# Feed forward on 512 moving columns: gate and up by tokens, down past one load for both parts, and a pad of 96 bytes

## The chip, the core and the metric

The kernel runs on one core of a Trainium2 chip. TensorE multiplies matrices and accumulates in PSUM; VectorE, ScalarE and GpSimd work on elements; 16 DMA engines move data from HBM into SBUF. The metric is the device time of one execution in microseconds, the median over several. In the profiles PE is TensorE's matmuls, PEld its loads of the stationary operand, DVE VectorE, ACT ScalarE, POOL GpSimd, SP the engine that issues the DMAs. A difference in this kernel's time under about 0.2% can't be told from none.

## The reference, cut to what matters

Two blocks of two layers each work on 256 tokens of 1024 features. The mixers (attention, recurrences, long convolutions) differ; each of the four layers ends with a gated feed forward of 2816 hidden features. In block 1, where `ffn_w_up` holds the gate's columns and then up's:

```python
hf = rmsnorm(x, norm_ffn)
gate, up = jnp.split(hf @ ffn_w_up, 2, axis=-1)
return x + (jax.nn.silu(gate) * up) @ ffn_w_down
```

Block 2 computes `(silu(u @ w1) * (u @ w3)) @ w2`, with u the modulated norm, and adds it times a gate per feature. All is float32.

## The kernel before, in words

The stream `xT` stands feature-major: 128 partitions, 8 tiles of features, 256 tokens. A float32 product is made of three products in the format fp32r: the weights are split into a high part `wh` (a ScalarE cast, L471) and a low part `wl` (a VectorE subtract, L472), the activations likewise, and `mm3` (L484 to L487) adds `wh` by high, `wh` by low and `wl` by high.

`weights` (L456) brings the weights in units of 512 KB: 4 blocks of 128 rows by 256 columns, into four buffers for what is loaded and three each for `wh` and `wl`. The layout of the weights in HBM is made in `layout` from the table TILES.

`s_tiles` (L489) computes 256 columns of weights for 256 tokens in one bank of PSUM: for each block k of 128 rows and each half of the columns, `mm3` with the 128 x 128 weights loaded and the 256 tokens moving. So every matmul of the feed forward moves 256 columns and has a load of its own. `t_form` (L508) is the other way round, tokens loaded and 256 weights' columns moving.

`ffn` (L537) runs over 11 tiles of 256 hidden features: gate into one bank, up into another, silu on ScalarE (L559), the product on VectorE (L560), and a split into `ph` and `pl` (L453, L454), feature-major already. In block 1 the norm's factor of each token is broadcast over the partitions (`pb`) and both products are multiplied by it (L555). In block 2 the first tile comes ready from `ffn_ahead`. Then four tiles of 256 output features: 22 blocks of hidden features, the same three products, and `residual` (L571 to L577) adds each half, 256 columns, to `xT`. Three banks of PSUM (tag mm) are shared by all of these.

The order on each engine is not the order of the code: the framework lays the whole program out by a simulated timeline and puts on each engine's queue what it thinks ready first, so work of other stages (in block 1 the contexts of block 2, called by `beside`) stands between the feed forward's matmuls.

Of the kernel before, what the change touches and what calls it, by code (L numbers as in the profile page):

```python
# [15 lines left out]
OP = mybir.AluOpType  # L16
# [106 lines left out]
def _dft():  # L123
    """Transforms at the frequencies pi (2 k + 1) / 512, k = 0..127 and then 255..128, of signals about 127.5 (F, and
    back: G) and, for k < 128, of the even and the odd places of the filters (H)."""
# [20 lines left out]
def _positions():  # L146
    """What the filters take of their places: the even ones, then the odd ones."""
# [27 lines left out]
def _run(c0, n, w=256):  # L175
    return [(c, [(c, w)]) for c in range(c0, c0 + n * w, w)]


# the weights in tiles of columns, which name or first column leads to: [pieces: first column or None, columns]
# [4 lines left out]
    "w_lift": _run(0, 4), "w_out": _run(0, 4), "ffn_w_up": _run(0, 22), "ffn_w_down": _run(0, 4),  # L184
# [3 lines left out]
    "ffn_w1_2": _run(0, 11), "ffn_w3_2": _run(0, 11), "ffn_w2_2": _run(0, 4),  # L188
# [11 lines left out]
def _unit(cols):  # L200
    """How many blocks of 128 rows one load brings, of how many columns at most."""
    return (KU, 256) if cols > 128 else (2 * KU, 128)


def layout(inputs):
    """The inputs as the chip loads them: vectors as columns, weights by tiles and units of rows, tokens turned."""
# [11 lines left out]
    for name in ("x", "mem", "ctx_2"):  # L218
        out[name + "_T"] = np.ascontiguousarray(inputs[name][0].reshape(S, KT, 128).transpose(2, 1, 0)).reshape(128, KT * S)
    for name, tiles in TILES.items():  # L220
# [3 lines left out]
        for _, pieces in tiles:  # L224
            cut = [w[:, :, c:c + n] if c is not None else np.zeros(w.shape[:2] + (n,), w.dtype) for c, n in pieces]
            t = cut[0] if len(cut) == 1 else np.concatenate(cut, 2)
            step = 256 if name == "mod_w_2" else _unit(t.shape[2])[0] * 128
# [8 lines left out]
class Halves:  # L236
    """Two [128, 4, tokens] tiles as one [128, 8, tokens]."""
# [13 lines left out]
class K:  # L251
# [22 lines left out]
    def pump(self, n=1):  # L274
        """Emit some of the work that waits to be laid between the matrix products."""
        self.due += n * self.rate
        while self.bg is not None and self.due >= 1:
            self.due -= 1
            self.pump_one()
# [57 lines left out]
    def later(self, *dst):  # L337
        """Whatever is loaded into dst waits until the first products are on their way."""
# [7 lines left out]
    def rstd_tokens(self, src, r, lp):  # L346
        """1 / rms of every token, per token, in r [128, 2]."""
# [9 lines left out]
    def rstd(self, src, pt):  # L357
        """1 / rms of every token, per token, with pt's first columns for the sums."""
# [43 lines left out]
    def s_ahead(self, u, at, bank="mm", mws=((0, 128), (128, 128)), t=None):  # L402
        """The tile that s_tiles gives, from what is ahead of the norm; in SBUF."""
# [23 lines left out]
    def norm_ahead(self, u, src, bank="aux2"):  # L427
        """The norm itself, after what is ahead of it."""
# [27 lines left out]
    def weights(self, name, i, key, kt=KT):  # L456
        """A function of k that gives high and low parts of rows k * 128.. of a tile; k must not go down."""
# [30 lines left out]

    def s_tiles(self, ps, at, xh, xl, kt=KT, first=True, last=True, x0=0, mws=((0, 128), (128, 128)), k0=0):  # L489
        """ps [m, 256 tokens each] += (columns m0..m0 + mw of the weights)^T x.  # L490

        Where sums of one bank are built up side by side only the bank's first product starts and only its
        last one stops."""
# [33 lines left out]
    def ffn_ahead(self, u, l, w_gate, w_up, u0, lp):  # L527
        """The first tile of the gated products."""
# [8 lines left out]
    def ffn(self, xh, xl, l, w_gate, w_up, u0, w_down, gcol=None, first=None, scale=None):  # L537
        nc = self.nc
        with self.pool("ffn") as fp:
            ph = fp.tile([128, FT, S], F32R, name="ph")  # L540
            pl = fp.tile([128, FT, S], F32R, name="pl")
            for i in range(FFN // 256):
# [3 lines left out]
                else:  # L546
                    pg = self.mm()
                    self.s_tiles(pg, self.weights(w_gate, l, i * 256), xh, xl)
                    pu = self.mm()
                    self.s_tiles(pu, self.weights(w_up, l, u0 + i * 256), xh, xl)  # L550
                    sg = fp.tile([128, 512], F32, tag="f1", bufs=2, name="f1")
                    pr = fp.tile([128, 512], F32, tag="f2", bufs=2, name="f2")
                    if scale is not None:
                        for o, ps in ((sg, pg), (pr, pu)):
                            nc.vector.tensor_tensor(o.rearrange("p (m t) -> p m t", m=2),  # L555
# [1688 lines left out]
```

## Time and profile before

| | |
|---|---|
| median of 3 runs | 2064.69 us (2064.21 to 2064.89) |
| span of the profiled execution (the only time that the page gives of it) | 2068.7 us |
| TensorE busy (16,666 matmuls) | 2030.9 us, 98% |
| VectorE, ScalarE busy | 1506.7 us (73%), 1033.8 us (50%) |
| chain that ended last | TensorE 92% |

The span is that of an execution under the profiler, 4.0 us above the median. Busy time counts a matmul's record from start to end; the records overlap, so the time that one matmul takes of the queue is the distance between two starts, which a count over a stretch gives. The feed forwards lie at about 431 to 660 us (with other work between), 1029 to 1286 (likewise), 1587 to 1742 and 1884 to 2059.

### The profile page before, as it was taken

To read this page: it belongs to the slowest core of one execution; us is meant where nothing else is said; L and a number is where in the kernel's file an instruction comes from. 1 tells how busy PE (TensorE), PEld (TensorE's weight loads), DVE (VectorE), ACT (ScalarE), POOL (GpSimd) and SP (SyncE) were. 2 spreads that over 40 slices of the span, in tenths; PEclk is the share of its full clock that TensorE was granted. 3 is DMA by queue.
4 is the path that set the end of the run, shared out by engine and by line. 5 is a ranking of instruction groups with operands and counts; after the bars stand their busy time and mean duration, and the time that the engine had idled before them with its cause. 6 is when DMAs were issued, how large, how long until landed. Compare 5 with 4: busy or idle time off the path is not lost.

```text
span 2068.7 us, 40596 instructions
## 1 busy us (share of the span) xinstructions
PE 2030.9 (98%) x16666; PEld 1931.3 (93%) x16666; DVE 1506.7 (73%) x2491; ACT 1033.8 (50%) x1604; POOL 86.7 (4%) x80
## 2 busy tenths in 40 slices
PE   8999999999999999999999999999989999999998
PEld 8999999999999989999999989897779999899998
DVE  6968877896866868977767855885667556897554
ACT  6553355565544664454655434662135445656443
POOL 0000000010000000000000001000010000001001
PEclk9999999999999999999999999997999999999999
DMA  8754564865567755747644534452215666545654
GB/s 323 273 179 156 201 204 167 319 244 193 185 220 241 239 169 174 243 144 263 201 160 145 175 109 141 164 159 80 67 47 177 194 187 222 163 133 176 190 176 132
DMA packets 118561, 379.34 MB, mean 183 GB/s; under 512 B 18239, under 2 KB 28776, under 8 KB 117096
## 3 DMA queue, kind: packets, MB, share of 16 engines
q1 hardware_dynamic: 118376, 376.76, 55.2%
q8 instruction: 130, 2.13, 0.4%
q14 instruction: 55, 0.45, 0.1%
HBM read 366.27 MB, written 10.25 MB: 182 GB/s over the span
## 4 chain that ended last, share of the span: by engine, by line
PE 92%; DVE 2%; ACT 2%; issue 2%; DMA 1%; POOL 0%; SPq 0%; DVEq 0%; POOLq 0%; ACTq 0%
PE mm L487 22%; PE mm L485 22%; PE mm L486 22%; PE mm L522 1%; PE mm L521 1%; PE mm L523 1%; PE aux L1233 1%; DVE wl L472 1%; PE aux L1758 1%; ACT wh L471 1%; PE aux L1085 1%; PE aux L1763 1%; PE aux L823 1%; PE aux L858 1%; PE aux L2094 1%
## 5 line engine op out<-in xcount | busy, mean ns | idle before, releaser
L471 ACT CAST wh<-w 128x1024 fp32r<-128x1024 f32 (+2 forms) x570 | 589.0, 1035 | 680.5 <-PE mm L486 521.7
L472 DVE TENSOR_TENSOR wl<-w,wh 128x1024 fp32r<-128x1024 f32 (+2 forms) x570 | 686.2, 1205 | 305.8 <-ACT wh L471 303.4
L485 PE MATMUL mm<-hh,wh 128*128 128x256 f32 (+1 forms) x1776 | 505.6, 285 | 1.3 <-ACT wh L471 0.7
L487 PE MATMUL mm<-hh,wl 128*128 128x256 f32 (+1 forms) x1776 | 504.1, 284 | 1.0 <-DVE wl L472 1.0
L486 PE MATMUL mm<-hl,wh 128*128 128x256 f32 (+1 forms) x1776 | 504.2, 284 | 0.0
L485 PEld LDWEIGHTS mm<-hh,wh 128*128 128x128 f32 (+1 forms) x1776 | 335.8, 189 | 6.0 <-issue 3.6
L487 PEld LDWEIGHTS mm<-hh,wl 128*128 128x128 f32 (+1 forms) x1776 | 335.7, 189 | 5.5 <-issue 3.3
L486 PEld LDWEIGHTS mm<-hl,wh 128*128 128x128 f32 (+1 forms) x1776 | 335.8, 189 | 3.9 <-issue 2.6
L485 PE MATMUL mm<-xh,wh 128*128 128x256 f32 x960 | 270.6, 283 | 1.0 <-ACT uc L422 0.9
L487 PE MATMUL mm<-xh,wl 128*128 128x256 f32 x960 | 269.5, 282 | 1.6 <-DVE wl L472 1.5
L486 PE MATMUL mm<-xl,wh 128*128 128x256 f32 x960 | 270.3, 283 | 0.2
L487 PE MATMUL mm<-ph,wl 128*128 128x256 f32 x704 | 197.9, 281 | 0.0
L485 PE MATMUL mm<-ph,wh 128*128 128x256 f32 x704 | 197.7, 281 | 0.0
L486 PE MATMUL mm<-pl,wh 128*128 128x256 f32 x704 | 197.4, 280 | 0.0
L487 PEld LDWEIGHTS mm<-xh,wl 128*128 128x128 f32 x960 | 182.2, 190 | 5.2 <-issue 2.5
L485 PEld LDWEIGHTS mm<-xh,wh 128*128 128x128 f32 x960 | 181.1, 189 | 4.1 <-issue 2.2
L486 PEld LDWEIGHTS mm<-xl,wh 128*128 128x128 f32 x960 | 180.5, 189 | 3.8 <-issue 3.0
L1227 DVE SCALAR_TENSOR_TENSOR macc<-mw,cs,macc 128x512 f32<-128x512 f32 x196 | 146.2, 752 | 10.8 <-DMA mw<-in_t_mod_w 10.2
L487 PEld LDWEIGHTS mm<-ph,wl 128*128 128x128 f32 x704 | 132.7, 189 | 1.9 <-issue 1.9
L485 PEld LDWEIGHTS mm<-ph,wh 128*128 128x128 f32 x704 | 132.4, 188 | 1.6 <-issue 1.5
L486 PEld LDWEIGHTS mm<-pl,wh 128*128 128x128 f32 x704 | 132.4, 188 | 1.5 <-issue 1.4
L487 PE MATMUL mm<-brh,wl 128*128 128x256 f32 x384 | 108.3, 283 | 0.0
(679 smaller groups left out, 3607.8 us busy)
## 6 DMA issues: line engine op xcount, KB each, us to landing
w<-in_t_w_in SPq DMA_DIRECT2D x148, 512.0 KB, 4.3
w<-in_t_ffn_w SPq DMA_DIRECT2D x128, 512.0 KB, 4.3
mw<-in_t_mod_w SPq DMA_DIRECT2D x96, 512.0 KB, 4.6
w<-in_t_ffn_w_up SPq DMA_DIRECT2D x88, 512.0 KB, 4.0
w<-in_t_ab_w_in SPq DMA_DIRECT2D x42, 512.0 KB, 4.9
w<-in_t_ffn_w_down SPq DMA_DIRECT2D x40, 512.0 KB, 3.6
w<-in_t_w_lift SPq DMA_DIRECT2D x32, 512.0 KB, 4.1
w<-in_t_hy_w_in SPq DMA_DIRECT2D x24, 512.0 KB, 4.2
```

The costliest lines, as they stand in the source:

```text
L471: nc.scalar.copy(wh, w)
L472: nc.vector.tensor_tensor(wl, w, wh, OP.subtract)
L485: nc.tensor.matmul(ps, wh, xh, start=start, stop=False)
L486: nc.tensor.matmul(ps, wh, xl, start=False, stop=False)
L487: nc.tensor.matmul(ps, wl, xh, start=False, stop=stop)
L521: nc.tensor.matmul(o, h, wh, start=(k + tb == 0), stop=False)
L522: nc.tensor.matmul(o, h, wl, start=False, stop=False)
L523: nc.tensor.matmul(o, l, wh, start=False, stop=(k == KT - 1 and tb == 1))
L823: nc.tensor.matmul(ps[:, jj * S:jj * S + ns], iqr[64 * u:64 * u + 64, j, tb * 128:(tb + 1) * 128], kr[64 * u:64 * u + 64, 1, :ns], start=T ...
L858: nc.tensor.matmul(ps[:, jj * S:jj * S + ns], qr[r, 2 * jp + jj, tb * 128:(tb + 1) * 128], kr[r, 0, :ns], start=True, stop=True)
L1085: nc.tensor.matmul(ps[64 * u:64 * u + 64, o + full:o + full + 32], k, q[:, full:full + 32], start=True, stop=True)
L1227: nc.vector.scalar_tensor_tensor(acc, v[:, k, :], sc, acc, op0=OP.mult, op1=OP.add)
```

## The change

Gate and up: `t_pair` takes 256 columns of the gate and the 256 of up that belong to them, side by side, as 512 moving columns, past 128 tokens loaded; one bank of PSUM holds 128 tokens. So the weights of gate and up are stored side by side (`_gated`), and a unit is 2 blocks of 128 rows by 512 columns, of the same 512 KB. Silu and product are taken per 128 tokens, with the norm's factor of a token as a scalar of its partition (block 1). The product is then turned by four f32 transposes on TensorE (128 x 128, into another bank), and the split reads that bank.

Down: `ph` and `pl` become the two halves of one tile `pp`, and `s_pair` moves both, 512 columns, past one load of `wh`; `wl` by the high part remains a matmul of 256 columns. One bank holds 128 output features in two halves, which `residual` adds one after the other, so it is called four times a tile.

The pad: a tile of 24 float32 per partition, never used, in the pool that holds `sin`, `cos` and `rx`. In the built programs the tiles of block 1 that come after it start 96 bytes later: `hh` at byte 82272 of a partition before (32 past a multiple of 64) and at 82368 now (a multiple of 64); the branches' tiles `brh` and `brl` likewise. The feed forward's `pp` in block 1 stands 32 past a multiple of 64, as `ph` and `pl` did. In block 2 `xh`, `xl`, `ph` and `pp` stand at multiples of 64 in both programs, at the same places.

```diff
+def _gated(i0):
+    return [(("g", i), [(i * 256, 256), (FFN + i * 256, 256)]) for i in range(i0, FFN // 256)]
...
 def _unit(cols):
-    return (KU, 256) if cols > 128 else (2 * KU, 128)
+    return (KU // 2, 512) if cols > 256 else (KU, 256) if cols > 128 else (2 * KU, 128)
...
+    def t_pair(self, ps, at, xh, xl):
+        nc = self.nc
+        ku = KU // 2
+        for k0 in range(0, KT, ku):
+            for tb in range(2):
+                for k in range(k0, k0 + ku):
+                    wh, wl = at(k)
+                    h, l = (x[:, k, tb * 128:(tb + 1) * 128] for x in (xh, xl))
+                    nc.tensor.matmul(ps[tb], h, wh, start=(k == 0), stop=False)
+                    nc.tensor.matmul(ps[tb], h, wl, start=False, stop=False)
+                    nc.tensor.matmul(ps[tb], l, wh, start=False, stop=(k == KT - 1))
+
+    def s_pair(self, ps, at, x, kt):
+        nc = self.nc
+        for k in range(kt):
+            wh, wl = at(k)
+            for m in range(2):
+                c = slice(m * 128, (m + 1) * 128)
+                nc.tensor.matmul(ps[m], wh[:, c], x[:, :, k, :], start=(k == 0), stop=False)
+                nc.tensor.matmul(ps[m][:, S:], wl[:, c], x[:, 0, k, :], start=False, stop=(k == kt - 1))
...
-    def ffn(self, xh, xl, l, w_gate, w_up, u0, w_down, gcol=None, first=None, scale=None):
+    def ffn(self, xh, xl, l, w_gated, w_down, gcol=None, first=None, r=None, bank="aux"):
...
-                    pg = self.mm()
-                    self.s_tiles(pg, self.weights(w_gate, l, i * 256), xh, xl)
-                    pu = self.mm()
-                    self.s_tiles(pu, self.weights(w_up, l, u0 + i * 256), xh, xl)
...
+                    ps = [self.mm(), self.mm()]
+                    self.t_pair(ps, self.weights(w_gated, l, ("g", i)), xh, xl)
+                    sg = fp.tile([128, 2, 256], F32, tag="f1", bufs=2, name="f1")
+                    pr = fp.tile([128, 2, 256], F32, tag="f2", bufs=2, name="f2")
+                    for tb in range(2):
+                        g, u = ps[tb][:, :256], ps[tb][:, 256:]
+                        if r is None:
+                            nc.scalar.activation(sg[:, tb, :], g, AF.Silu)
+                            nc.vector.tensor_tensor(pr[:, tb, :], sg[:, tb, :], u, OP.mult)
+                        else:
+                            nc.scalar.activation(sg[:, tb, :], g, AF.Silu, scale=r[:, tb:tb + 1])
+                            nc.vector.scalar_tensor_tensor(pr[:, tb, :], u, r[:, tb:tb + 1], sg[:, tb, :], op0=OP.mult,
+                                                           op1=OP.mult)
+                    with self.banks(bank):
+                        pt = self.aux()
+                    for m in range(2):
+                        for tb in range(2):
+                            nc.tensor.transpose(pt[:, m * S + tb * 128:m * S + (tb + 1) * 128],
+                                                pr[:, tb, m * 128:(m + 1) * 128], self.ident)
+                    prv = pt.rearrange(M2, m=2)
...
-                pd = self.mm()
-                self.s_tiles(pd, self.weights(w_down, l, i * 256, FT), ph, pl, FT)
+                pd = [self.mm(), self.mm()]
+                self.s_pair(pd, self.weights(w_down, l, i * 256, FT), pp, FT)
                 for m in range(2):
-                    self.residual(2 * i + m, pd[:, m * S:(m + 1) * S], gcol)
+                    for part in range(2):
+                        self.residual(2 * i + m, pd[m][:, part * S:(part + 1) * S], gcol)
...
+            rp.tile([128, 24], F32, name="rpad")
```

TensorE's queue in the last feed forward, before: the end of up (xh and xl moving) and the start of down (ph and pl moving), each matmul 256 columns wide.

```order
L486 MATMUL mm_22970<-xl_21510,wh_23002 128x256
L487 MATMUL mm_22970<-xh_21509,wl_23003 128x256
L485 MATMUL mm_22970<-xh_21509,wh_23002 128x256
L486 MATMUL mm_22970<-xl_21510,wh_23002 128x256
L487 MATMUL mm_22970<-xh_21509,wl_23003 128x256
L485 MATMUL mm_23037<-ph_21753,wh_23039 128x256
L486 MATMUL mm_23037<-pl_21754,wh_23039 128x256
L487 MATMUL mm_23037<-ph_21753,wl_23040 128x256
```

The same queue now, in the last tile of gate and up: mm_20683 and mm_20684 are its two halves of tokens, f2_20671 the product of the tile before, aux_20676 the bank that it is turned into.

```order
L506 MATMUL mm_20684<-wh_20704,xl_19654 128x512
L504 MATMUL mm_20684<-wh_20704,xh_19653 128x512
L505 MATMUL mm_20684<-wl_20705,xh_19653 128x512
L506 MATMUL mm_20684<-wh_20704,xl_19654 128x512
L595 MATMUL aux_20676<-cst_72,f2_20671 128x128 x3
L504 MATMUL mm_20683<-wh_20722,xh_19653 128x512
L504 MATMUL mm_20684<-wh_20722,xh_19653 128x512
L505 MATMUL mm_20683<-wl_20723,xh_19653 128x512
L506 MATMUL mm_20683<-wh_20722,xl_19654 128x512
```

The transposes stand inside the next tile: the first of the four after 12 of its matmuls, all of its first half of tokens, and the other three, shown here, after 12 more, of its second half.

The same queue now in down, where mm_20770 and mm_20771 are the two banks of one tile.

```order
L516 MATMUL mm_20770<-pp_19897,wh_20817 128x512
L517 MATMUL mm_20770<-pp_19897,wl_20818 128x256
L516 MATMUL mm_20771<-pp_19897,wh_20817 128x512
L517 MATMUL mm_20771<-pp_19897,wl_20818 128x256
L516 MATMUL mm_20770<-pp_19897,wh_20817 128x512
```

Wide and narrow matmuls take turns, and the tile fills two banks at once where it filled one.

VectorE's queue where one tile of the last down is handed on, before: wl are the weights of the tiles that follow, fy belongs to the final norm.

```order
L472 TENSOR_TENSOR wl_23211<-w_23209,wh_23210 128x1024
L472 TENSOR_TENSOR wl_23241<-w_23239,wh_23240 128x1024
L576 SCALAR_TENSOR_TENSOR xT_73<-mm_23037,mod1_81,xT_73 128x256 x2
L472 TENSOR_TENSOR wl_23271<-w_23269,wh_23270 128x1024
L2163 TENSOR_SCALAR fy_23729<-xT_73,P_74 128x256 x2
```

And now:

```order
L478 TENSOR_TENSOR wl_20904<-w_20902,wh_20903 128x1024
L613 SCALAR_TENSOR_TENSOR xT_73<-mm_20770,mod1_81,xT_73 128x256
L478 TENSOR_TENSOR wl_20926<-w_20924,wh_20925 128x1024
L613 SCALAR_TENSOR_TENSOR xT_73<-mm_20771,mod1_81,xT_73 128x256
L613 SCALAR_TENSOR_TENSOR xT_73<-mm_20770,mod1_81,xT_73 128x256
L478 TENSOR_TENSOR wl_20948<-w_20946,wh_20947 128x1024
L613 SCALAR_TENSOR_TENSOR xT_73<-mm_20771,mod1_81,xT_73 128x256
L2204 TENSOR_SCALAR fy_21298<-xT_73,P_74 128x256 x2
```

Two residuals became four, with weight subtracts between them.

## Rows read from the trace of the kernel before

**Rows 1.** The page: span, busy time of the engines, slices, chain.
```profile
span 2068.7 us, 40596 instructions
...
PE 2030.9 (98%) x16666; PEld 1931.3 (93%) x16666; DVE 1506.7 (73%) x2491; ACT 1033.8 (50%) x1604; POOL 86.7 (4%) x80
...
PEclk9999999999999999999999999997999999999999
...
PE 92%; DVE 2%; ACT 2%; issue 2%; DMA 1%; POOL 0%; SPq 0%; DVEq 0%; POOLq 0%; ACTq 0%
```

**Rows 2.** Waits of TensorE, longest first: total, times, longest, in us.
```profile
PE mm L521 <- ACT memh L597: 9.4, 1, 9.4
PE aux L1846 <- DVE do L1837: 4.9, 2, 3.8
PE mm L2042 <- POOL fb L2036: 2.7, 2, 1.5
PE mm L487 <- DVE wl L472: 2.7, 5, 1.0
```

**Rows 3.** Stretches: busy us and count of PE, PEld, DVE, ACT, POOL; clock; DMA.
```profile
610.00:650.00 40.00, 40.00 (x341) 40.00 (x340) 29.27 (x37) 19.50 (x27) 5.05 (x5) 1.00 0.74 254
1600.00:1680.00 80.00, 80.00 (x708) 80.00 (x707) 44.87 (x44) 38.57 (x45) 0.00 (x0) 1.00 0.64 193
...
1910.00:1990.00 80.00, 80.00 (x681) 80.00 (x681) 43.41 (x43) 37.23 (x43) 0.00 (x0) 1.00 0.60 187
2005.00:2025.00 20.00, 20.00 (x172) 20.00 (x171) 9.52 (x12) 8.14 (x10) 1.20 (x1) 1.00 0.59 182
2045.00:2055.00 10.00, 10.00 (x91) 10.00 (x90) 6.21 (x8) 3.54 (x5) 2.20 (x2) 1.00 0.09 28
```

**Rows 4.** Timeline at an f32 matmul (start, length in us); its mean by form.
```profile
800.83 0.28 PE L487 MATMUL mm<-hh,wl 128*128 128x256 f32 x1
800.95 1.03 PE L747 MATMUL aux<-bk,cst 128*128 128x256 f32 x4
...
L747 PE MATMUL aux<-bq,cst 128*128 128x256 f32 x16 | 4.1, 378 | 0.0
```

**Rows 5.** Timeline around four f32 transposes; their mean by form.
```profile
1827.02 0.28 PE L485 MATMUL mm<-xh,wh 128*128 128x256 f32 x1
1827.13 0.28 PE L486 MATMUL mm<-xl,wh 128*128 128x256 f32 x1
1827.26 0.60 PE L2068 MATMUL aux<-cst,hsd 128*128 128x128 f32 x4
1827.61 0.36 PE L487 MATMUL mm<-xh,wl 128*128 128x256 f32 x1
1827.81 0.28 PE L485 MATMUL mm<-xh,wh 128*128 128x256 f32 x1
...
L2068 PE MATMUL aux<-cst,hsd 128*128 128x128 f32 x32 | 4.8, 273 | 0.0
```

**Rows 6.** Timeline of matmuls past 72 loaded columns; loads of 128 and 72.
```profile
747.03 0.28 PE L487 MATMUL mm<-hh,wl 128*72 128x256 f32 x1
747.15 0.28 PE L485 MATMUL mm<-hh,wh 128*72 128x256 f32 x1
747.27 0.28 PE L486 MATMUL mm<-hl,wh 128*72 128x256 f32 x1
747.39 0.28 PE L487 MATMUL mm<-hh,wl 128*72 128x256 f32 x1
...
L485 PEld LDWEIGHTS mm<-hh,wh 128*128 128x128 f32 x1760 | 333.5, 189 | 6.0 <-issue 3.6 <-ACT wh L471 0.9 <-ACT bq L765 0.8
...
L485 PEld LDWEIGHTS mm<-hh,wh 128*72 128x72 f32 x16 | 2.3, 142 | 0.0
```

**Rows 7.** VectorE and ScalarE by line and form: busy us, mean ns, idle before.
```profile
L472 DVE TENSOR_TENSOR wl<-w,wh 128x1024 fp32r<-128x1024 f32 x550 | 672.0, 1223 | 288.0 <-ACT wh L471 285.6 <-PE mm L487 0.5
L555 DVE TENSOR_TENSOR f<-mm,pb 128x512 f32<-128x512 f32 x44 | 30.3, 688 | 19.1 <-PE mm L487 18.9
...
L576 DVE SCALAR_TENSOR_TENSOR xT<-mm,mod,xT 128x256 f32<-128x256 f32 x32 | 13.9, 476 | 9.6 <-PE mm L487 9.6
...
L574 DVE TENSOR_TENSOR xT<-xT,mm 128x256 f32<-128x256 f32 x32 | 12.0, 415 | 3.5 <-PE mm L487 3.2
...
L471 ACT CAST wh<-w 128x1024 fp32r<-128x1024 f32 x550 | 576.3, 1050 | 649.8 <-PE mm L486 491.2 <-issue 77.6 <-PE mm L523 27.6
...
L363 ACT ACTIVATE sq<-xT 128x256 f32<-128x256 f32 x64 | 25.8, 404 | 7.8 <-DVE xT L576 7.8
```

More of the change, by code (lines that the diff above doesn't have):

```diff
@@ L183 @@
         ("k", [(O_DK, 64), (O_DK, 64), (O_IK, 64), (O_IK, 64)]), ("v", [(O_DV, 64), (O_IW, 8)])],
-    "w_lift": _run(0, 4), "w_out": _run(0, 4), "ffn_w_up": _run(0, 22), "ffn_w_down": _run(0, 4),
+    "w_lift": _run(0, 4), "w_out": _run(0, 4), "ffn_w_up": _gated(0), "ffn_w_down": _run(0, 4),
     "mod_w_2": _run(0, 12, 512),
@@ L187 @@
     "ab_w_out_2": _run(0, 4), "hy_w_in_2": _run(0, 12), "hy_w_out_2": _run(0, 4),
-    "ffn_w1_2": _run(0, 11), "ffn_w3_2": _run(0, 11), "ffn_w2_2": _run(0, 4),
+    "ffn_w1_2": _run(0, 1), "ffn_w3_2": _run(0, 1), "ffn_w13_2": _gated(1), "ffn_w2_2": _run(0, 4),
 }
@@ L219, in layout @@
         out[name + "_T"] = np.ascontiguousarray(inputs[name][0].reshape(S, KT, 128).transpose(2, 1, 0)).reshape(128, KT * S)
+    inputs = {**inputs, "ffn_w13_2": np.concatenate([inputs["ffn_w1_2"], inputs["ffn_w3_2"]], 2)}
     for name, tiles in TILES.items():
@@ L226, in layout @@
             t = cut[0] if len(cut) == 1 else np.concatenate(cut, 2)
-            step = 256 if name == "mod_w_2" else _unit(t.shape[2])[0] * 128
+            step = _unit(t.shape[2])[0] * 128
             for r in range(0, t.shape[1], step):
@@ L535, in ffn_ahead @@
         return pr
-    def ffn(self, xh, xl, l, w_gate, w_up, u0, w_down, gcol=None, first=None, scale=None):
+    def ffn(self, xh, xl, l, w_gated, w_down, gcol=None, first=None, r=None, bank="aux"):
         nc = self.nc
+        M2 = "p (m t) -> p m t"
         with self.pool("ffn") as fp:
-            ph = fp.tile([128, FT, S], F32R, name="ph")
-            pl = fp.tile([128, FT, S], F32R, name="pl")
+            pp = fp.tile([128, 2, FT, S], F32R, name="pp")
             for i in range(FFN // 256):
@@ L546, in ffn @@
                 else:
-                    pg = self.mm()
-                    self.s_tiles(pg, self.weights(w_gate, l, i * 256), xh, xl)
-                    pu = self.mm()
-                    self.s_tiles(pu, self.weights(w_up, l, u0 + i * 256), xh, xl)
[L551 to L555, printed above, removed]
-                                                    ps.rearrange("p (m t) -> p m t", m=2),
-                                                    scale[:, None, :].to_broadcast([128, 2, S]), OP.mult)
-                        pg, pu = sg, pr
@@ L559, in ffn @@
-                    nc.scalar.activation(sg, pg, AF.Silu)
-                    nc.vector.tensor_tensor(pr, sg, pu, OP.mult)
-                    prv = pr.rearrange("p (m t) -> p m t", m=2)
-                self.split(prv, ph[:, 2 * i:2 * i + 2, :], pl[:, 2 * i:2 * i + 2, :])
+                    ps = [self.mm(), self.mm()]
+                    self.t_pair(ps, self.weights(w_gated, l, ("g", i)), xh, xl)
+                    sg = fp.tile([128, 2, 256], F32, tag="f1", bufs=2, name="f1")
+                    pr = fp.tile([128, 2, 256], F32, tag="f2", bufs=2, name="f2")
@@ new lines, in ffn @@
+                    with self.banks(bank):
[5 more added lines that the diff above has]
+                    prv = pt.rearrange(M2, m=2)
+                self.split(prv, pp[:, 0, 2 * i:2 * i + 2, :], pp[:, 1, 2 * i:2 * i + 2, :])
@@ L1170, in b1_layer @@
             with self.pool("ff") as lp:
-                pb = lp.tile([128, S], F32, name="pb")
+                r = lp.tile([128, 2], F32, name="fr")
                 g = self.col("norm_ffn", l * 8, 8)
@@ L1174, in b1_layer @@
                     self.split_scaled(self.xT[:, k, :], g[:, k:k + 1], hh[:, k, :], hl[:, k, :])
-                nc.scalar.copy(pb, self.rstd_bcast(self.xT))
+                with self.banks("aux2"):
+                    pt = self.aux()
+                nc.vector.tensor_copy(r, self.rstd(self.xT, pt)[:, :2])
                 if l == 0:
@@ L1181, in b1_layer @@
                 self.rate = RATES[3]
-                self.ffn(hh, hl, l, "ffn_w_up", "ffn_w_up", FFN, "ffn_w_down", scale=pb)
+                self.ffn(hh, hl, l, "ffn_w_up", "ffn_w_down", r=r, bank="aux2")
             self.tap(f"xl{l}", self.xT)
@@ L1959, in ffn2 @@
                 self.dft_loads()
-            self.ffn(xh, xl, i, "ffn_w1_2", "ffn_w3_2", 0, "ffn_w2_2", gcol=self.mod[i][:, 40:48], first=pr)
+            self.ffn(xh, xl, i, "ffn_w13_2", "ffn_w2_2", gcol=self.mod[i][:, 40:48], first=pr)
         self.tap(f"hl{i}", self.xT)
```

## The prediction

> **What bounds the kernel now.** I read the page first. TensorE is busy 98% of the span and its clock stands at the full level in nearly every slice [rows 1]; the chain that ended last is TensorE for 92% [rows 1]. The waits of TensorE come next: the longest is 9.4 us at the start of the program, and no line of the feed forward (L485 to L487 with ph, pl, or the gate and up products) waits for more than 2.7 us in all [rows 2]. So the kernel is as long as its queue of matmuls, and the change is worth what it does to the time between two matmul starts. A matmul's own record is of no use for that: it is 0.28 us long while the next starts 0.12 us later [rows 6]. I therefore count matmuls in stretches that hold nothing but the feed forward [rows 3]; since some 2.4 records reach in from before the stretch (0.28 over 0.118), I take that many off.
> - Block 1, down, 610 to 650 us: (341 - 2.4) in 40 us, 118.1 ns each.
> - Block 2 layer 0, gate and up, 1600 to 1680: 113.4 ns.
> - Block 2 layer 1, gate and up, 1910 to 1990: 117.9 ns; down begins like that (2005 to 2025: 117.9) and ends at 112.9 to 113 (2045 to 2055), so 115.6 on the whole.
>
> The clock is at its 2.4 GHz level in all of them, where 256 columns, one a cycle, are 106.7 ns. So every matmul of 256 columns carries 6.7 to 11.4 ns that are not columns. The change removes half of the gate and up matmuls and a third of the down matmuls, not their columns: what it can win is those nanoseconds.
>
> **Gate and up.** Before, 2 x 1056 (block 1) + 2 x 960 (block 2, whose first tile is made ahead) = 4032 matmuls: 2112 x 118.1 + 960 x 113.4 + 960 x 117.9 = 249.4 + 108.9 + 113.2 = 471.5 us. After, 2016 of 512 columns. No fp32r matmul of 512 columns is in the trace, so its price is bounded. From below, 216 ns: the f32 matmul L747 spends (1.03 - 0.38) / 3 = 217 ns on a pass of 256 columns, 512 cycles, each with a load of 128 columns beside it [rows 4]. From above, 2 x 118 = 236 ns: what comes on top of the columns could grow with the columns. Against the upper end speaks that the extra seems tied to the matmul: with 72 loaded columns in place of 128 the load's record falls from 189 to 142 ns, and the matmuls still start 0.12 us apart [rows 6], so it is not the loaded columns that cost. I take 220: the f32 row's 216 and the 4 ns by which an fp32r matmul of 256 columns at its best (113.4) stands above an f32 instruction of as many cycles (109, below). 2016 x 220 = 443.5 us: a gain of 28.0 us (36 at 216, -4.3 at 236).
>
> **Down.** Before 2112 matmuls: 1056 x 118.1 + 528 x 113.4 + 528 x 115.6 = 245.6 us. After, 704 of 512 columns (both parts of the product past one load) and 704 of 256. The wide ones read two runs of 256 columns, in block 1 from places 32 bytes past a multiple of 64, so I add 2 ns: 222. The narrow ones stay at their layer's spacing: 352 x 118.1 + 176 x 113.4 + 176 x 115.6 = 81.9. With 704 x 222 = 156.3 that is 238.2: a gain of 7.4 us (13.7 at 216 and 113.4, -2.4 at 236).
>
> **Transposes, new.** 42 tiles x 4 = 168 f32 transposes of 128 columns. The trace has this form in L2068: four of them with (0.60 - 0.27) / 3 = 109 ns between starts, and L485, which without them would start at about 1827.37, starts at 1827.81: 0.44 us for four, 110 ns each [rows 5]. Split as one and three, as the order has them, they cost the same by that count. 168 x 110 = 18.5 us, all on TensorE's path. The Trainium skill (TensorE: Matmul & The Clock Gate, Part 4: PE-mode transpose) has about 275 ns for a transpose inside a kernel. That is the length of L2068's record (273), not its spacing. By the page the term would be 46 us and the sum a loss of some 7 us; the trace decides, and I keep 18.5.
>
> **The pad.** 96 bytes move everything of block 1 that comes after it from 32 bytes past a multiple of 64 to a multiple of 64. Outside the feed forward that is 4656 matmuls: 3216 with hh and hl moving, 288 with them loaded, 1152 with the branches' tiles. They now take 118.1 by the nearest pure stretch. What the trace has at multiples of 64 is 113.4 in one layer and 117.9 in the other, with tiles at the same places; within the last down it changes from the one to the other [rows 3]. So the place alone doesn't decide, and I take the middle of 0.2 and 4.7 ns, 2.5 ns: 11.6 us (bounds 0.9 and 21.9).
>
> **What it adds beside the matmuls.** The residual is now four VectorE instructions a tile instead of two, at 0.42 to 0.48 us [rows 7]. Inside a layer they lie beside matmuls. At the end of each of the four layers the next norm waits for them: 4 x 2 x 0.45 = 3.6 us. At each tile's end ScalarE, VectorE and then the transposes follow each other. In block 2 the order puts 12 wide matmuls of the next tile, 12 x 0.22 = 2.64 us, in front of the first transpose, and 12 more in front of the other three. The chain is a silu of 256 columns (0.40 by the row of that size), a weight subtract of 1.22 that may have just begun on VectorE, and the product (0.42): 2.0 us, hidden. If ScalarE also has just begun a weight cast (1.05), it is 3.1 us and TensorE waits 0.45 us. Behind the transpose stand the matmuls of the tile's second half, which other weights' buffers wait for. I take this for one tile in five: 42 x 0.45 / 5 = 3.8 us. The two products with the norm's factor (44 x 0.69 on VectorE in block 1) and its broadcast go; TensorE waited for neither, so nothing. DMAs are as many and as large as before.
>
> **Sum.** 28.0 + 7.4 - 18.5 + 11.6 - 3.6 - 3.8 = 21.1 us off the profiled execution's 2068.7. That span is 4.0 us above the median of the runs, 2064.7, and the lines of the sum are 0.2% off by as much at most, so I take the gain off the median: 2043.6, say 2043 us.
>
> **Rivals.**
> - *The extra goes with the columns.* 512 columns take 236 ns. For it: at one place 113.4 and 117.9 both occur, so the extra isn't a plain fixed cost of a matmul, and nothing of 512 fp32r columns is shown. Against it: rows 4 and 6. Then gate and up lose 4.3, down 2.4, the transposes 18.5, ends and waits 7.4, and the pad gives 11.6: 21 us slower, 2086. It decides from about 228 ns on: 2720 wide matmuls x 7.8 ns are the whole gain.
> - *All of the extra goes.* 216 ns wide and 113.4 in all that the pad moves: 36.0 + 13.7 - 18.5 + 21.9 - 3.6 = 49.5 us, 2015. For it, the one layer that runs at 113.4 throughout; against it, the other. A rule of the Trainium skill (TensorE: Matmul & The Clock Gate, Back-to-back issue gap) would make a matmul of 512 columns 216 ns too, but by it one of 256 takes 109, and rows 3 have 113 to 118; its 2.5 ns of fixed cost would leave nothing to win here.
> - *The tile's end becomes a wait.* Every one of the 42 tiles waits 0.45 us, and the bank handed on in down, which needs four residuals with 1.2 us subtracts between them (1.8 + 1.2 = 3.0 against 8 x (222 + 117) = 2.7 us of cover), adds 0.3 us x 12: 15.1 more than 3.8 is 18.7 in all, gain 2 to 6 us, 2060. For it, VectorE and ScalarE run their queues in order; against it, they are busy under 60% in block 2's stretches [rows 3].
>
> **How the numbers follow.** Forecast 0.57, all of the extra goes 0.13, wait at the tile's end 0.15, by the columns 0.12, the rest (a slower place for another stage, since the order of the whole program is made anew) 0.03. A difference under 0.2% (4.1 us) can't be told from none. Faster: 0.56 of the forecast, 0.13, 0.12 of the wait: 0.81. Same: 0.07. Slower: 0.12. The range runs from 2014 to 2060; the case by the columns is left out.
>
> **What would show it.** In the changed profile: a stretch of gate and up in block 2 with one matmul per 220 ns (80 us with about 355 and the transposes); L595 in fours at 110 ns; block 1's 256-column stretches below 118; no wait of TensorE for f2 above 4 us in all. It is wrong if 512 columns take over 228 ns, or if L595 waits for VectorE at most tiles.

## The result, and the profile after

The change made the kernel slower. Medians on one chip, run in turn:

| | median | lowest to highest | runs |
|---|---|---|---|
| before | 2064.8 us | 2061.1 to 2073.9 | 6 |
| after | 2081.4 us | 2079.3 to 2082.8 | 6 |

The ratio after/before is 1.0057, 95% interval 1.0029 to 1.0084: about 12 us, between 6 and 17. The medians themselves lie 16.6 us apart, at the upper end of that. The profiled executions differ by 12.0: 2068.7 us before, 2080.7 after. The forecast was 2043 us (range 2014 to 2060). The 0.2% named at the start as what can be told apart is too small: 35 runs of the kernel before, beside the first experiments, lie between 2059.5 and 2084.3 us, and the intervals below are 0.2 to 0.4% wide on either side.

The page of the changed kernel (the same lines of before are [rows 1]):

```profile
span 2080.7 us, 35557 instructions
...
PE 2038.9 (98%) x14106; PEld 1814.6 (87%) x14106; DVE 1493.8 (72%) x2523; ACT 1044.7 (50%) x1647; POOL 85.2 (4%) x80
...
PEclk9999899999999999999999999997989999999999
```

TensorE has 2560 instructions less than before (16666 to 14106) and is still busy 98% of a span that is 12 us longer. Instructions went, time didn't. It isn't waits either; those of TensorE after, longest first (total, times, longest, in us) [rows 2]:

```profile
PE mm L551 <- ACT memh L634: 8.5, 1, 8.5
PE aux L1887 <- DVE do L1878: 4.9, 2, 3.9
PE mm L552 <- DVE wl L478: 3.7, 2, 2.5
PE mm L493 <- DVE wl L478: 3.0, 4, 1.1
...
PE mm L517 <- DVE wl L478: 1.2, 1, 1.2
...
PE mm L2206 <- DVE xT L613: 1.1, 1, 1.1
...
PE mm L504 <- ACT wh L477: 0.2, 1, 0.2
```

The new code is at L504 to L506 (gate and up), L595 (transposes), L516 and L517 (down). Its waits are the last rows, 2.5 us with the end of the program (L2206); L595 never waits. So, as in the prediction, the time lies between the starts of two matmuls, and the stretches show it [rows 3]. Two stretches of gate and up of block 2, all instructions:

```profile
1600.00:1680.00 80.00, 80.00 (x366) 65.38 (x365) 43.85 (x50) 37.45 (x49) 0.00 (x0) 1.00 0.59 184
1910.00:1990.00 80.00, 80.00 (x365) 65.41 (x364) 43.96 (x49) 37.33 (x50) 0.00 (x0) 1.00 0.60 186
```

The same stretches with L595 alone (TensorE's busy time and count, clock, DMA):

```profile
1600.00:1680.00 80.00, 5.19 (x29) 1.00 0.59 184
1910.00:1990.00 80.00, 5.32 (x28) 1.00 0.60 186
```

Some 1.7 records reach in from before each stretch (0.39 over 0.229). 366 - 29 - 1.7 = 335.3 wide matmuls in 80 us less 29 transposes at 0.11: 229 ns each, and 229 in the other stretch too. The forecast was 220; from 228 on the whole gain was to be gone. In block 1 they are slower still. Timeline there (start and length in us), 12 wide matmuls from the first row shown to the last:

```profile
499.89 0.39 PE L504 MATMUL mm<-wh,hh 128*128 128x512 f32 x1
500.13 0.39 PE L505 MATMUL mm<-wl,hh 128*128 128x512 f32 x1
500.36 0.39 PE L506 MATMUL mm<-wh,hl 128*128 128x512 f32 x1
...
502.69 0.39 PE L504 MATMUL mm<-wh,hh 128*128 128x512 f32 x1
```

2.80 us over 12: 233.3 ns, against 2 x 118.1 = 236 for the two matmuls of 256 columns that each of them replaces. And down in block 2, wide and narrow in turn, ten of each from the first row to the last:

```profile
2035.89 0.40 PE L516 MATMUL mm<-pp,wh 128*128 128x512 f32 x1
2036.12 0.28 PE L517 MATMUL mm<-pp,wl 128*128 128x256 f32 x1
2036.24 0.40 PE L516 MATMUL mm<-pp,wh 128*128 128x512 f32 x1
...
2039.42 0.39 PE L516 MATMUL mm<-pp,wh 128*128 128x512 f32 x1
```

3.53 us over ten: 353 ns for a pair. The forecast was 222 for the wide one and 113 to 118 for the narrow one; what it replaced, three matmuls of 256 columns, took 340 to 354.

The transposes in the same layer (a group of one, then one of three):

```profile
1633.86 0.40 PE L506 MATMUL mm<-wh,xl 128*128 128x512 f32 x1
1634.09 0.27 PE L595 MATMUL aux<-cst,f 128*128 128x128 f32 x1
1634.12 0.48 PE L504 MATMUL mm<-wh,xh 128*128 128x512 f32 x1
1634.43 0.39 PE L505 MATMUL mm<-wl,xh 128*128 128x512 f32 x1
...
1636.73 0.40 PE L506 MATMUL mm<-wh,xl 128*128 128x512 f32 x1
1636.97 0.49 PE L595 MATMUL aux<-cst,f 128*128 128x128 f32 x3
1637.21 0.70 PE L504 MATMUL mm<-wh,xh 128*128 128x512 f32 x2
1637.75 0.39 PE L505 MATMUL mm<-wl,xh 128*128 128x512 f32 x1
```

From L506 to the L505 behind the transpose are 0.57 us where two wide matmuls take 0.46: 0.11 for one transpose (L504 starts 0.03 behind it and the matmul after pays the rest). From 1636.73 to 1637.75 are 1.02 us where three wide ones take 0.69: 0.33 for three. This is [rows 5] again.

By stage, from the timelines of both (a feed forward counts from its first gate or up matmul to the last of down, with what the planner lays between; block 2's first runs from 1571 us before):

| us | before | after |
|---|---|---|
| feed forward, block 1, two layers | 487.4 | 487.4 |
| feed forward, block 2, two layers | 345.6 | 354.4 |
| all the rest | 1235.7 | 1238.9 |

Block 2's 345.6 has one layer at 113.4 ns a matmul and one at 117.9 [rows 3]; in other executions of the same code both stand at 113 (shown under Places), and then these two layers take about 340 us. The rest got no faster in spite of the pad. A part of that is the clock:

```profile
core 0: 2068.7 us, clock 0.982
```

before, and after:

```profile
core 0: 2080.7 us, clock 0.979
```

The granted clock has two levels, 1.2 and 2.4 GHz. A mean of 0.982 is 0.018 / 0.5 x 2068.7 = 74 us at the lower one, 0.979 is 87 us; if TensorE works through the 13 us more, they cost half of that, some 6 us (an estimate). None of the low stretches lies in a feed forward in either profile. How much there is of them differs from run to run of one kernel: the mean clock of the 35 runs of the kernel before goes from 0.974 to 0.986.

### The profile page after: what moved, and what is told of

Its sections match the earlier page's. It is cut to its first block, busy times and chain, and to the rows that moved or that the text cites. A ratio compares the mean times of both kernels' runs of the same rounds, so it can differ in the third digit from the quotient of the medians.

```text
span 2080.7 us, 35557 instructions
## 1 busy us (share of the span) xinstructions
PE 2038.9 (98%) x14106; PEld 1814.6 (87%) x14106; DVE 1493.8 (72%) x2523; ACT 1044.7 (50%) x1647; POOL 85.2 (4%) x80
## 4 chain that ended last, share of the span: by engine, by line
PE 70%; DVE 4%; issue 2%; ACT 2%; DMA 1%; POOL 0%; SPq 0%; DVEq 0%; POOLq 0%; ACTq 0%
PE mm L504 7%; PE mm L505 7%; PE mm L506 7%; PE mm L516 7%; PE mm L493 6%; PE mm L492 6%; PE mm L491 6%; PE mm L517 4%; DVE wl L478 1%; PE aux L595 1%; PE mm L2083 1%; PE aux L1799 1%; PE aux L1804 1%; PE aux L491 1%; PE aux L2135 1%
## 5 line engine op out<-in xcount | busy, mean ns | idle before, releaser
L491 PE MATMUL mm<-hh,wh 128*128 128x256 f32 (+1 forms) x1072 | 305.8, 286 | 2.4 <-ACT hh L447 1.2
L493 PE MATMUL mm<-hh,wl 128*128 128x256 f32 (+1 forms) x1072 | 305.8, 286 | 1.0 <-DVE wl L478 1.0
L492 PE MATMUL mm<-hl,wh 128*128 128x256 f32 (+1 forms) x1072 | 305.4, 285 | 0.2
L516 PE MATMUL mm<-pp,wh 128*128 128x512 f32 x704 | 248.3, 398 | 0.0
L493 PEld LDWEIGHTS mm<-hh,wl 128*128 128x128 f32 (+1 forms) x1072 | 204.1, 190 | 4.5 <-issue 2.6
L517 PE MATMUL mm<-pp,wl 128*128 128x256 f32 x704 | 193.1, 282 | 1.2 <-DVE wl L478 1.2
L516 PEld LDWEIGHTS mm<-pp,wh 128*128 128x128 f32 x704 | 129.7, 188 | 28.1 <-issue 1.2
L505 PE MATMUL mm<-wl,hh 128*128 128x512 f32 x352 | 140.2, 398 | 0.0
L506 PE MATMUL mm<-wh,hl 128*128 128x512 f32 x352 | 139.6, 397 | 0.0
L517 PEld LDWEIGHTS mm<-pp,wl 128*128 128x128 f32 x704 | 132.0, 188 | 6.8 <-issue 1.9
L504 PE MATMUL mm<-wh,hh 128*128 128x512 f32 x352 | 137.7, 403 | 0.2 <-ACT wh L477 0.2
L506 PE MATMUL mm<-wh,xl 128*128 128x512 f32 x320 | 124.0, 393 | 0.0
L505 PE MATMUL mm<-wl,xh 128*128 128x512 f32 x320 | 124.0, 391 | 0.0
L504 PE MATMUL mm<-wh,xh 128*128 128x512 f32 x320 | 118.5, 401 | 0.0
```

Of the source, the lines that this page charges most:

```text
L491: nc.tensor.matmul(ps, wh, xh, start=start, stop=False)
L492: nc.tensor.matmul(ps, wh, xl, start=False, stop=False)
L493: nc.tensor.matmul(ps, wl, xh, start=False, stop=stop)
L504: nc.tensor.matmul(ps[tb], h, wh, start=(k == 0), stop=False)
L505: nc.tensor.matmul(ps[tb], h, wl, start=False, stop=False)
L506: nc.tensor.matmul(ps[tb], l, wh, start=False, stop=(k == KT - 1))
```

## The experiments

Theory at the start: the step that failed is the price of a wide matmul; it grows with its columns, and so the transposes are a net loss. Rival: the wide matmuls do gain, and something else (the new order, transposes dearer than their spacing, the pad) takes it back.

**The pad alone** (12 runs).

```
 the kernel before, and in block1():
+            rp.tile([128, 24], F32, name="rpad")
```

> The kernel before with the 96-byte pad alone. Theory (an fp32r matmul of 512 columns costs as much as two of 256, so the change gives only the pad's gain and pays for the transposes): the pad works, and all fp32r matmuls of block 1, feed forward included, go from 118.2 to about 116.6 ns as the mixers' did in the changed kernel: some 7800 x 1.6 = 12 us faster, 2053 us. Rival (the pad's shift does nothing by itself; the mixers' 116.6 came with the new order of the program): 2065 us, block 1 stays at 118.

Measured: 2065.7 against 2069.1 us, ratio 0.9978 (0.9955 to 1.0001). That is 4.6 us, at most 9, where the prediction's term had 11.6 for a part of these matmuls alone, and the 12 expected here did not come; that the pad gives nothing is just inside the interval. The traces show that it does something. Block 1's down and block 2's second gate and up in this kernel:

```profile
610.00:650.00 40.00, 40.00 (x343) 40.00 (x342) 29.30 (x38) 19.45 (x27) 5.06 (x5) 1.00 0.73 249
...
1910.00:1990.00 80.00, 80.00 (x708) 80.00 (x708) 45.48 (x44) 37.82 (x44) 0.00 (x0) 1.00 0.60 196
```

In block 1 (343 - 2.4) in 40 us are 117.4 ns, 118.1 before. The second row has 113.4 ns where [rows 3] have 117.9, though the pad moves nothing in block 2; I come back to that under Places. The runs of this kernel also spent longer at 1.2 GHz (mean clock 0.978 against 0.981 of the kernel before beside it, some 12 us more), so the 4.6 us are what was left after that loss.

**The changed kernel without transposes** (10 runs). It leaves the turn out and splits the product as it stands.

```
-                    with self.banks(bank):
-                        pt = self.aux()
-                    for m in range(2):
-                        for tb in range(2):
-                            nc.tensor.transpose(...)
-                    prv = pt.rearrange(M2, m=2)
+                    prv = pr
```

> The changed kernel without its 168 transposes (the product is split without being turned, so the feed forward's second half is computed from features in the wrong places). Theory: the transposes cost TensorE 110 ns each and nothing else, 18.5 us: 2081 - 18.5 = 2063 us. Rival (the loss is not in the transposes but in what surrounds them: order, clock, waits at the tile's end): under 6 us faster, 2076 or more. A second rival (transposes also stretch the matmuls around them): over 25 us faster, below 2056.

Measured: 2064.5 us, ratio 0.9979 (0.9956 to 1.0002). The profiled span is 2063.4, 17.3 us under that of the changed kernel: 103 ns for each of 168 transposes, where 110 were forecast. The two executions differ in the clock too (0.982 against 0.979), so the spans alone don't price a transpose; block 2's feed forwards, at full clock in both, take 354.4 us with their 80 transposes and 345.3 without, 0.11 us each. The stretch of gate and up in this kernel, which has no transpose in it:

```profile
1910.00:1990.00 80.00, 80.00 (x352) 65.63 (x351) 45.66 (x51) 39.09 (x51) 0.00 (x0) 1.00 0.61 195
```

80 / (352 - 1.7) = 228 ns: the wide matmuls are as slow without transposes between them. Without its transposes the change is worth no more than the pad alone.

**Gate and up alone, down alone** (12 runs each).

```
 gate and up alone: the changed kernel with
-                pd = [self.mm(), self.mm()]
-                self.s_pair(pd, ..., pp, FT)
+                pd = self.mm()
+                self.s_tiles(pd, ..., pp[:, 0], pp[:, 1], FT)
 (and two residuals); down alone: the kernel before with pad, pp and s_pair
```

> Gate and up by tokens with transposes and the pad, down as in the kernel before. Theory: down's wide matmuls (233 ns) and narrow ones (118) give back nothing against three of 256 at 116 to 118, so undoing that part takes 2 to 5 us off: 2077 us. Rival (down past one load is a gain that the gate and up part hides): 2085 us or more.

> The kernel before with the pad and the change of down alone. Theory: as fast as the pad alone or 1 to 4 us slower, since 233 + 118 is not less than three times 117, and four residuals stand at each end: 2053 to 2058 us. Rival (the loads saved are worth something): 5 us faster than the pad alone.

Measured: gate and up alone 2078.3 us, 1.0057 (1.0033 to 1.0081), as slow as the whole change; down alone 2068.9, 1.0000 (0.9975 to 1.0024), some 3 us above the pad alone. So down's part gives nothing and costs little, and the loss is that of gate and up with its transposes. Undoing down was to take 2 to 5 us off; by the ratios it took nothing off. By stages it goes both ways: in this kernel block 1's two feed forwards take some 5 us more than in the changed one (down's matmuls of 256 columns start 120 to 121 ns apart there, 118 in the kernel before) and block 2's some 5 us less (114 ns). Down alone stands 11 us or more above its 2053 to 2058, since that number took the pad at its forecast worth.

**One price by itself** (one execution). Behind the end of the kernel before, groups of 30 like fp32r matmuls, each group behind one tiny f32 matmul (L2181).

```
+            def group(n, m0=0, s0=1024, sw=128, two=False):
+                nc.tensor.matmul(pb[:, :1], self.ident, self.ones[:, :1], start=True, stop=True)
+                ...
+                for _ in range(30):
+                    nc.tensor.matmul(pb[:sw, :n], q[:, s0:s0 + sw], mv, start=True, stop=True)
```

> The kernel before, and behind its end 13 groups of 30 fp32r matmuls each on one tile, back to back, between them one f32 matmul of one column: 128, 256, 384 and 512 columns; then 256 and 512 each with the moving start 32 bytes on, with the loaded start 32 bytes on, with the moving start 64 bytes on, and with 64 loaded columns; last 512 columns in two runs of 256. Theory (the stream runs at 17 cycles for 16 columns at 2.4 GHz, and a matmul has at most some 10 ns of its own): 256 take 113 to 118, 384 about 170 to 175, 512 about 227 to 232, with 64 loaded columns the same; 32 bytes off adds some ns. Rival (a fixed cost a matmul of 7 to 11 ns over one column a cycle, and what the changed kernel shows at 512 is contention with its neighbours): 384 take 167, 512 take 220. The prediction went by the rival.

The timeline of the first groups (128, 256, 384 and 512 columns):

```profile
2060.20 3.55 PE L2184 MATMUL mm<-mq 128*128 128x128 f32 x30
2063.58 0.33 PE L2181 MATMUL mm<-cst 128*128 128x1 f32 x2
2063.77 3.84 PE L2184 MATMUL mm<-mq 128*128 128x256 f32 x30
2067.45 0.28 PE L2181 MATMUL mm<-cst 128*128 128x1 f32 x2
2067.59 5.45 PE L2184 MATMUL mm<-mq 128*128 128x384 f32 x30
2072.88 0.28 PE L2181 MATMUL mm<-cst 128*128 128x1 f32 x2
2073.02 7.07 PE L2184 MATMUL mm<-mq 128*128 128x512 f32 x30
2079.93 0.28 PE L2181 MATMUL mm<-cst 128*128 128x1 f32 x2
```

From a group's start to the L2181 behind it are 30 intervals, of which the first is longer by some 0.09 us (0.20 at 256 columns, 0.32 at 512). So 512 columns take (6.91 - 0.32) / 29 = 227 ns, 384 take 173, 256 here 120, 128 take 112. From 256 to 384 and from 384 to 512 columns 54 ns are added each time, for 128 columns that are 53.3 at one a cycle of 2.4 GHz. So at this place 256, 384 and 512 columns carry 13, 13 and 14 ns on top of their columns: here the extra is nearly fixed per matmul, as the prediction argued, but it is 13 and not 7. At other places it isn't fixed: with the moving operand 32 bytes further on 256 take 117 and 512 take 233 (10 and 20 on top), with the loaded one 32 bytes further on 118 and 233, with the moving one 64 bytes further on 118 and 229. With 64 loaded columns in place of 128, which were to change nothing, 256 take 117 and 512 take 230; 512 in two runs of 256 take 227. No group of 512 came below 227, though nothing but like matmuls stood around it, so the rival of this run (220) is out. The f32 row's 217 ns for 512 cycles, on which the forecast leaned, holds for passes of an f32 matmul and not for 512 fp32r columns. The Trainium skill (TensorE: Matmul & The Clock Gate, Back-to-back issue gap) gives a fixed 2.5 ns on top of the columns as the gap of an isolated matmul, 216 ns here; no group shows that, and the measurement decides.

But 256 columns at 120, on multiples of 64 bytes, was more than in any layer of the kernel, and 64 bytes on they took 117.8. That asked for the next.

**Places** (one execution): 256 columns at other places, and the same places again behind tiny matmuls of other sizes.

```
-            def group(n, m0=0, s0=1024, sw=128, two=False):
+            def group(n, m0=0, s0=1024, gap=1, alt=0):
+            for gap in (1, 2, 3, 5, 7, 9):
+                group(256, gap=gap)
+            ...
+            for m0 in (16, 32, 48):
+                group(256, m0=m0)
+            for s0 in (1040, 1056, 1072):
+                group(256, s0=s0)
+            group(256, m0=32, s0=1056)
```

> The kernel before, with 20 groups of 30 like fp32r matmuls behind its end (its time is that of the program plus about 75 us). Each group begins with a small f32 matmul of 1 to 9 columns, and its operands stand 0, 64, 128 or 192 bytes further on. Theory A, a matmul of 256 columns has two spacings, 113.3 and 117.8 ns, and which of them a run of matmuls falls into depends on the places of its operands: the six groups at the same places agree within 0.5 ns, and the groups at other places differ from them. Theory B, it depends on when the run begins: the groups at the same places fall into different spacings (some near 113, some near 117 to 120), whatever their places. Both: 512 columns never below 226 ns.

The groups with the moving operand 64, 128 and 192 bytes further on:

```profile
2105.98 3.78 PE L2184 MATMUL mm<-mq 128*128 128x256 f32 x30
2109.59 0.28 PE L2181 MATMUL mm<-cst 128*128 128x1 f32 x2
2109.73 3.81 PE L2184 MATMUL mm<-mq 128*128 128x256 f32 x30
2113.38 0.28 PE L2181 MATMUL mm<-cst 128*128 128x1 f32 x2
2113.52 3.65 PE L2184 MATMUL mm<-mq 128*128 128x256 f32 x30
2117.01 0.28 PE L2181 MATMUL mm<-cst 128*128 128x1 f32 x2
```

117.6, 119.0 and 113.4 ns (first interval 0.20 us again). From the other groups' starts: with the loaded operand moved instead by 64, 128 and 192 bytes 113.3, 118.6 and 117.8; with both moved by 128 bytes 120.0; six times at the first place, whatever stood ahead, 119.7 to 120.0. The rows are rounded, so these are good to some 0.4 ns. Theory A holds in the groups, and more narrowly: what counts is how far the moving operand stands from the loaded one, modulo 256 bytes (moving 192 on and loaded 64 on agree, so do moving 64 on and loaded 192 on). Whether it is the operand just loaded or the one loaded next, these runs don't tell. Best is 64 bytes back, 113.3 ns. Block 2 of the kernel before stands there (moving tiles at 64, weights at 128, modulo 256), its block 1 32 bytes back (96 and 128; 118.3), and the 96-byte pad brought block 1 to 64 bytes on, which is one of the worse places.

In the kernel the place isn't all. The stretch of block 2's second gate and up that has 681 matmuls in [rows 3], in this run, whose program is the kernel before up to its end; then block 2's first gate and up in the run of down alone, whose `xh` and `xl` lie where they lay before:

```profile
1910.00:1990.00 80.00, 80.00 (x709) 80.00 (x708) 45.64 (x44) 37.91 (x44) 0.00 (x0) 1.00 0.60 196
...
1600.00:1680.00 80.00, 80.00 (x681) 80.00 (x680) 43.90 (x43) 36.54 (x42) 0.00 (x0) 1.00 0.61 186
```

So at one place, 64 bytes back, a layer stands at 113.2 ns in one profile and at 117.9 in another, through the whole stretch. What puts it there stays open.

**The changed kernel without its pad** (5 runs): the one line goes.

> The changed kernel without its 96-byte pad: block 1's tiles go back to 32 bytes past a multiple of 64. Theory (the pad alone gave the kernel before about 4.5 us, and wide matmuls 32 bytes off took 6 ns more): some 1400 wide matmuls of block 1 stand at 233 ns already, so they lose nothing, and the mixers lose 1.5 ns on 4656 matmuls: 2086 to 2089, ratio to before 1.009. Rival, the pad is worth its predicted 11.6 us within the changed kernel: 2093. Rival, the pad is worth nothing: 2081.

Measured: 2082.5 us, 1.0098 (1.0058 to 1.0138); span 2080.5, where the changed kernel had 2080.7. The interval overlaps with that of the changed kernel, so this run tells the rivals of 2081 and 2086 us not apart; nor does the ratio exclude 11.6 us, and one span of each kernel decides little where runs of this one lie between 2080 and 2097 us. What the traces show is the spacing: where the mixers' matmuls of 256 columns (`hh`, `hl` or the branches' tiles moving) follow each other directly in block 1, they start 118.3 ns apart on the mean without the pad, as in the kernel before, and 116.8 with it. That is the 1.5 ns of the theory, 7 us over 4656 matmuls.

**A pad of 224 bytes**, in the kernel before (6 runs) and in the changed one (12 runs). It puts block 1 at 64 bytes back.

```
-            rp.tile([128, 24], F32, name="rpad")
+            rp.tile([128, 56], F32, name="rpad")
```

> The kernel before with a pad of 224 bytes in the place of the 96. Theory, what a matmul of 256 columns carries on top of its columns is set by how far its moving operand stands from the loaded operand of the next matmul, modulo 256 bytes (e6_places: 113.3 ns at 64 bytes back, 117.8 at 64 on, 118.7 at 128, 120.0 at 0; block 1 of the kernel before stands 32 bytes back and takes 118.3): with 224 bytes block 1 comes to 64 bytes back, and some 7500 matmuls go from 118.3 to 113.3 ns: 37 us off, about 2030, ratio 0.982. Rival, only being at a multiple of 64 counts: as with the 96 bytes, 117 ns and ratio 0.998. Rival, the spacing 113.3 does not last beside block 1's other work (its second layer in block 2 stood at 117.8): half, 2048, ratio 0.991.

> The changed kernel with a pad of 224 bytes in the place of its 96. Same theory: some 4440 matmuls of block 1's mixers go from 116.8 to 113.3 (15.5 us) and 930 wide ones, which now stand 64 bytes on, from 233.1 to 229.1 as in block 2 (3.7 us): 19 us off, 2062, ratio to before 0.998, and about 30 us above e8_pad_224, since the wide matmuls do not come below 2 x 113.5 ns and the transposes stay. Rival, a multiple of 64 counts alone: 2081, ratio 1.006. Rival, at a good place of block 1 the wide matmuls fall to 220 ns as predicted: another 12 us off, 2050.

Measured on one chip, beside each other: the kernel before with this pad 2051.2 us, ratio 0.9907 (0.9877 to 0.9938); the changed one 2077.0, 1.0035 (1.0015 to 1.0054). The first beats both kernels. Its page, and a stretch of block 1's gate and up and one of block 2's:

```profile
span 2042.3 us, 40596 instructions
...
PE 2003.9 (98%) x16666; PEld 1905.3 (93%) x16666; DVE 1504.5 (74%) x2491; ACT 1034.0 (51%) x1604; POOL 85.7 (4%) x80
...
560.00:600.00 40.00, 40.00 (x355) 40.00 (x354) 29.32 (x35) 17.35 (x20) 0.00 (x0) 1.00 0.69 223
...
1910.00:1990.00 80.00, 80.00 (x708) 80.00 (x707) 45.33 (x45) 37.79 (x45) 1.20 (x1) 1.00 0.60 191
```

40 / (355 - 2.4) = 113.4 ns in block 1, with the same 16666 matmuls; before it was 118.1 [rows 3]. The gain is 26 us by the spans, 19 (13 to 25) by the ratio, not the 37 expected: the mixers' matmuls in block 1, counted as above, went from 118.3 to 115.0 ns on the mean, 3.3 and not 5.0. By stages 9 us of the 26 are block 1's feed forwards, 13 the rest of the program, and 4 block 2's second layer, which the pad doesn't move. The mixers' mean goes by the place in every kernel: 118.3 at 32 bytes back (the kernel before, the changed one without pad), 116.9 and 116.8 at 64 on (the pad alone, the changed kernel), 115.0 and 115.0 at 64 back. So in block 1 the order of the places is that of the theory, the best place gives less than in the groups, and the third rival has the time.

The changed kernel's wide matmuls in block 1 with this pad, 12 from the first row to the last:

```profile
500.22 0.39 PE L504 MATMUL mm<-wh,hh 128*128 128x512 f32 x1
500.45 0.39 PE L505 MATMUL mm<-wl,hh 128*128 128x512 f32 x1
...
502.97 0.39 PE L504 MATMUL mm<-wh,hh 128*128 128x512 f32 x1
```

2.75 us over 12: 229 ns, as expected from block 2, and not 220. With the same pad in both, the change costs 25.9 us (2077.0 - 2051.2; 28.0 by the spans): more than with the pad that came with it. Matmuls of 256 columns win by the place (113.4 for 118.1 in block 1's feed forwards), wide ones less (229 for 233, where two of 256 would now take 227). A part is the clock again: these runs of the changed kernel have a mean of 0.976, those of the other 0.979, some 11 us more at 1.2 GHz, of which about half would be lost (an estimate).

## Why the prediction was wrong, point by point

- **What bounds the kernel**: right. TensorE's queue of matmuls is the time, in all versions.
- **Gate and up, the step that failed.** "I take 220", because "the extra seems tied to the matmul". Measured 233.3 in block 1 and 229 in block 2: 1056 x 233.3 + 960 x 229 = 466.2 us, a gain of 5.3 against 28.0. The price of 512 columns was the f32 row's 216 and 4 ns taken from the best layer's 113.4. That puts it 6.7 ns above the 213.3 of its columns, as 113.4 stands 6.7 above 106.7; but that extra belongs to one place and one width. In the groups 512 columns carry 14 to 20 ns, and 256 carry 7 to 13, each by its place: at distance 0 both carry some 13, at 32 bytes on 10 and 20. So the extra is neither a fixed cost of a matmul nor simply a share of the columns, and at no place tried is it 7 ns at 512. The argument from 72 loaded columns showed little: with 64 of them 256 columns took 3 ns less and 512 took 2 ns more. That one form takes 113.4 in one layer and 117.9 in the other, which the prediction named under the rival, was the better evidence. The gain of 5.3 itself leans on the 117.9 of the profiled execution; with 113.4 in both layers, as in other profiles, it is 1.0. The change also puts weights and tokens at other distances than before; distance 0, the groups' best for 512, was not tried in the kernel. By the groups' 227 it would give some 9 us more (an estimate), with the 5.3 still less than the transposes cost.
- **Down**: 704 pairs at about 352 are 247.8 us, a loss of 2.2 in place of a gain of 7.4. Same step; the pair is what three matmuls of 256 columns took.
- **Transposes**: right, 18.5 forecast; 0.11 us each in the timeline and in block 2's feed forwards without them, 17.3 by the spans. By the Trainium skill's 275 ns (TensorE: Matmul & The Clock Gate, Part 4: PE-mode transpose) the estimate would have been 46; the runs show that this is a length and not a price.
- **The pad**: right in sign, mis-sized: 2.5 ns a matmul forecast, 11.6 us; 1.5 by the spacings, 7.0 us; about 4.6 (-0.2 to 9.3) by the times of the pad alone, which have their own loss by the clock in them. The prediction looked at places modulo 64 of one operand; in the groups it is the distance of two operands modulo 256 that counts. It had both layers of block 2 at one place with two prices, and that is not settled: the second layer stood at 117.9 in the profiled kernel before, and at 113 in the four other profiles with this code for block 2 (708 or 709 records in the stretch that had 681), and in the run of down alone gate and up of both layers stood at 117.9.
- **Waits at tile ends and residuals** (7.4 us together): L595 never waits, the end of the program 1.1 us. Too dear by some 6 us. (VectorE, taken as busy under 60% in block 2's stretches, is at 62% in the last of [rows 3]; nothing came of it.)
- **Not forecast**: some 6 us from more time at 1.2 GHz in the profiled execution, by the estimate above. It comes with the pad alone as well.

Sum by the spacings and the clock of the two profiled executions: 5.3 - 2.2 - 18.5 + 7.0 - 1.1 - 6 = -15.5 us; the spans differ by -12.0, the ratio by -6 to -17. The terms are good to a few us. Of the rivals, "the extra goes with the columns" came nearest, with its mark of 228 ns passed, but not by its mechanism, which the groups at distance 0 contradict. Its 2086 us was 5 too high: it had 236 ns and the waits, too much loss, and the pad's 11.6, too much gain, so the closeness is partly luck.

## What to carry to other kernels

Fewer, wider matmuls win only what is fixed per instruction, so find out first whether the time above the columns is fixed: two widths of the same type, with their operands at the distances that they will have in the kernel, show it, and a row of another type (f32 passes) doesn't. Where a change buys width with extra instructions on the bounding engine, the extra ones are sure and the gain is not. Before restructuring a queue of matmuls that stand a few per cent above their columns, try where the operands lie: here one unused tile of 224 bytes gave 19 us, about what had been forecast for the whole restructuring.

## What the runs showed of the hardware that I had not expected

- fp32r matmuls of 256 columns take 113.3, 117.8, 118.7 or 120.0 ns at full clock, by the distance of the moving from the loaded operand modulo 256 bytes (64 back, 64 on, 128, 0), in groups of 30 on one tile. In the kernel a layer at 64 back can stand at 117.9 through a whole stretch of 80 us.
- 512 columns want another distance than 256: 227 at 0, 229 at 64 on, 233 at 32 either way, and 233 to 235 in the kernels' stretches that stood 64 back. At 0 the time above one column a cycle is the same 13 to 14 ns for 256, 384 and 512 columns; at 32 on it doubles from 256 to 512.
- 128 columns take 112 ns (at distance 0, where 256 take 120): twice the 53 ns of their columns.
